# Eight modulation rows of a two-layer diffusion backbone, gathered in one PSUM bank and turned once

## The chip, the cores and the metric

The kernel runs on one core of one Trainium2 chip. The metric is device time in microseconds, from the first to the last instruction of one execution. The median of three runs of the kernel before is 1852.27 us (1848.69 to 1852.5). A core has five engines that run side by side, each with its own queue of instructions in a fixed order: PE (TensorE, matrix products), DVE (VectorE), ACT (ScalarE), POOL (GpSimd) and SP (SyncE, here only the issuer of most transfers). PE multiplies from SBUF, the working memory of 128 partitions, into PSUM, eight banks of 512 fp32 columns by 128 partitions.

## What is computed

A backbone of two layers over 1024 latent tokens and 256 context tokens, width 1024: layer 0 is windowed attention, layer 1 a bidirectional state-space mixer. Every layer is modulated by two condition vectors, c for the latent tokens and c_ctx for the context tokens:

```python
def adaln(cond, w, b):
    mod = jax.nn.silu(cond) @ w + b
    return jnp.split(mod, 3, axis=-1)
...
for i in range(DEPTH):
    shift, scale, gate = adaln(c, w_ada[i], b_ada[i])
    shift_c, scale_c, gate_c = adaln(c_ctx, w_ada[i], b_ada[i])
    u = rms_normalize(h) * (1.0 + scale[:, None]) + shift[:, None]
    ...
    h = h + gate[:, None] * y
```

For each layer this is a product of 2 x 1024 by 1024 x 3072, so six blocks of 512 output columns: blocks 0 and 1 are the shift, 2 and 3 the scale, 4 and 5 the gate. The products are computed in fp32. What uses them wants a modulation value as one number per partition, with the 128 features of a tile on the partitions. A product comes out the other way round, as two rows (c and c_ctx) of 512 columns, and so has to be turned.

## The kernel before

Most matrix products are made in three passes from a split of each fp32 operand into a high part (wh, uH) and a rest (wl, uL). `mm3` (L223 to L229) issues them: high by high (L227), high by rest (L228), rest by high (L229). The weights arrive by a transfer (wr, L220), ACT casts them to the high part (L213), DVE or POOL subtracts (L215).

Blocks 0 to 3 of layer 0 are needed at once and are made at the start (`ada0`, L361 to L371, tiles wada and arow). The other eight, blocks 4 and 5 of layer 0 and all six of layer 1, are made later, between the projections of layer 0, by `adaln_col`. One block is eight transfers of 256 KB (L181, k = 0 to 7, alternately four in the buffers wh and four in wl of the pool wv) and eight matmuls (L185). The weight operand of such a matmul is 32 columns wide (`cs32`: two columns with silu of c and c_ctx, 30 of zeros), so that four matmuls of a group stand side by side in the array, each writing one strip of 32 partitions of the bank `aps`. Two groups, k = 0 to 3 and k = 4 to 7, make one block. Then comes the ninth step, `fin`: ACT copies the bank to SBUF (L189, a buffer of the tag qf), `modulation` turns it by four matmuls of 128 x 128 slices against `sel` (L201, which also adds the four strips), DVE adds the bias (L203), and, by the block, one more DVE operation (L192 or L205). fp32 matmuls show two records each in the profile: a group of four is eight records of L185, a turning eight records of L201.

Which engine's queue holds what in which order is decided by the framework. It plans the whole kernel in simulated time from the program's order, places an instruction where it thinks its operands are ready, picks the buffer of a tag and sets the semaphores. The program only says in which order the steps are written down. Around the change that is `qkvg` (L551 to L607): after the k and v projections it runs eight rounds of q projections (x = 0 to 7, for each the context tokens, i = 2, and then the first 512 latent tokens, i = 0) and eight of g projections (i = 2 for all x, i = 0 for x = 4 to 7), and calls `fill` after each projection, which runs the next three, three, three or two steps of the list `ada`. With nine steps to a block the list has 72 steps.

The projections use the two qf buffers too: `rope` for a q or k of latent tokens (L501 to L504) and `g_out` (L541 to L543, the last being the transfer of the result, sg, to memory). Behind the last projection the pools wv, wq and qp are closed and the attention's pools att, wo and qp1 are opened in the same place of SBUF. A new tile waits for the last users of the bytes under it. The attention starts with transfers of cos and sin (L510, L511), q (L614, L620, on POOL's queue), sg (L616), and the weights of the projections of the other 512 latent tokens (L220, cast at L213), which run between the attention's blocks.

Of the kernel before, what the change touches and what calls it, by code (L numbers as in the profile page):

```python
# [9 lines left out]
F32 = mybir.dt.float32  # L10
# [3 lines left out]
ALU = mybir.AluOpType  # L14
# [3 lines left out]
P = 128  # L18
D = 1024
KT = D // P  # L20
# [22 lines left out]
    pj=1, S=2, pt=2, pv=1,  # L43
# [60 lines left out]
class Kernel:  # L104
# [52 lines left out]
    def load_cond(self, p):  # L157
        nc, t, cp = self.nc, self.t, self.cp
        cc = t(p, [P, KT, 2], F32, "cc")
        nc.sync.dma_start(cc, self.a["cc"].rearrange("p (k c) -> p k c", k=KT))  # L160
        th = t(p, [P, KT, 2], F32, "cth")
        nc.scalar.activation(th, cc, AF.Tanh, scale=0.5)
        nc.vector.tensor_scalar_mul(cc, cc, 0.5)
        cs = self.csf = t(cp, [P, KT, 2], F32, "cs")
        nc.vector.scalar_tensor_tensor(cs, in0=th, scalar=1.0, in1=cc, op0=ALU.add, op1=ALU.mult)

        self.sel = t(cp, [P, 2], F32, "sel")
        nc.vector.tensor_reduce(self.sel, self.ident.rearrange("p (j r) -> p r j", r=32)[:, 0:2], axis=mybir.AxisListType.X, op=ALU.add)
        self.bada = t(cp, [P, 2, 24], F32, "bada")
        nc.sync.dma_start(self.bada, self.a["bada"].rearrange("p (l t) -> p l t", l=2))  # L170

    def adaln_col(self, layer, n, pool, ps):

        nc, t = self.nc, self.t
        st = {}

        def step(k):
            if k == 0:
                st["ps"] = t(ps, [P, 512], F32, "aps", 2)
            raw = t(pool, [P, 4, P], F32, ("wh", "wl")[k // 4])  # L180
            nc.sync.dma_start(raw, self.a["w_ada"][layer, n, k].rearrange("p (a c) -> p a c", a=4))  # L181
            st[k] = raw
            if k % 4 == 3:
                for j in range(4):
                    nc.tensor.matmul(st["ps"][32 * j : 32 * j + 32], self.cs[:, k - 3 + j, :], st[k - 3 + j].rearrange("p a c -> p (a c)"), start=k == 3, stop=k == KT - 1)  # L185

        def fin():
            row = t(self.pq, [P, 512], F32, "qf")
            nc.scalar.copy(row, st["ps"])  # L189
            m = self.modulation(layer, n, row, ps)  # L190
            if n // 2 == 2 and layer == 0:
                nc.vector.tensor_scalar_mul(m, m, 0.5)  # L192

        return [lambda k=k: step(k) for k in range(KT)] + [fin]

    def modulation(self, layer, n, row, ps):

        nc = self.nc
        mt = self.t(ps, [P, 512], F32, "pt")
        for j in range(4):  # L200
            self.last_mod = nc.tensor.matmul(mt[:, 2 * j : 2 * j + 2], row[:, j * P : (j + 1) * P], self.sel, start=True, stop=True)  # L201
        m = self.mod[layer][:, n * 4 : n * 4 + 4, :]
        nc.vector.tensor_tensor(m, mt[:, :8].rearrange("p (a b) -> p a b", b=2), self.bada[:, layer, n * 4 : n * 4 + 4].unsqueeze(2).broadcast_to([P, 4, 2]), op=ALU.add)  # L203
        if n // 2 == 1:
            nc.vector.tensor_scalar_add(m, m, 1.0)  # L205
        return m
# [91 lines left out]
    def layer0(self):  # L298
        nc, t, a = self.nc, self.t, self.a
        cps = ExitStack()  # L300
        BUFS.update(S=1, pj=4, wr=7, qf=2, ql=2, wh=4, wl=4, sqt=2)
        self.psA = self.pool("psA", space=PSUM, ctx=cps)
        NB = (LAT + CTX) // P
        self.uH, self.uL = [None] * 3, [None] * 3
        cw = ExitStack()
        wvp = self.pool("wv", ctx=cw)

        self.cs = t(wvp, [P, KT, 32], F32, "cs32")
        nc.vector.memset(self.cs, 0.0)
        nc.vector.tensor_copy(self.cs[:, :, 0:2], self.csf)  # L310
        self.wp = self.pool("wq", ctx=cw)
        p = self.pq = self.pool("qp", ctx=cw)
        c0 = ExitStack()
        self.q_d = [[t(self.dr, [4, 2, HD, n], F32, f"q{j}_{i}") for i, (_, n) in enumerate(TT)] for j in range(KV)]
        self.sg_d = [[t(self.dr, [2, P, n], F32, f"sg{j}_{i}") for i, (_, n) in enumerate(TT)] for j in range(KV)]
        wk, wv = self.norm0(c0, p, wvp)
        c0.close()
        ckv = ExitStack()
        kvp = self.pool("kv", ctx=ckv, side="right")
        self.kHH = [t(kvp, [P, LAT + CTX], F32R, f"kHH{j}") for j in range(KV)]  # L320
        self.v = t(kvp, [P, NB, KV, 2 * HD], F32R, "v")
        self.kL = [t(kvp, [P, LAT + CTX], F32R, f"kL{x}") for x in range(KV // 2)]
        self.mask = t(kvp, [P, 1152], BF16, "mask")
        self.nsink = t(kvp, [P, HEADS], F32, "nsink")
        self.sink = t(kvp, [P, HEADS], F32, "sink")
        self.qkvg(p, wk, wv, wvp)
        if "u" in self.dump:
            for i, (s, n) in enumerate(TT):
                self.dump_split("u", self.uH[i], self.uL[i], i, n, s)
        cw.close()  # L330
        cps.close()
        with ExitStack() as c1:
            BUFS.update(S=2, pj=1)
            self.psA = self.pool("psT", space=PSUM, ctx=c1)
            self.attention(c1, ckv)
            BUFS.update(pj=2)
# [24 lines left out]
    def ada0(self, n, raw, ps):  # L361

        nc, t = self.nc, self.t
        pj = t(ps, [P, 512], F32, "aps", 2)
        for k in range(KT):
            j = k % 4
            mm = nc.tensor.matmul(pj[32 * j : 32 * j + 32], self.cs[:, k, :], raw[k // 2][:, k % 2], start=k < 4, stop=k >= 4)
        row = t(self.p0, [P, 512], F32, "arow")
        nc.scalar.copy(row, pj)
        self.modulation(0, n, row, ps)  # L370
        return mm, self.last_mod  # L371
# [179 lines left out]
    def qkvg(self, p, wk, wv, wvp):  # L551
        nc, t, a = self.nc, self.t, self.a
        ps = self.psA
        nc.gpsimd.dma_start(self.mask, a["mask"])
        nc.sync.dma_start(self.sink, a["sink"].broadcast_to([P, HEADS]))
        nc.vector.tensor_scalar_mul(self.nsink, self.sink, -1.0)
        v = self.v
        NB = (LAT + CTX) // P
        kh_d = [[t(self.dr, [P, n], F32, f"k{x}_{i}") for i, (_, n) in enumerate(TT)] for x in range(2)]

        def kproj(x, i):
            s, n = TT[i]
            h, _ = self.qk(p, self.proj_h(ps, wk[x], self.uH, self.uL, i), i, self.kL[x][:, s : s + n])
            nc.sync.dma_start(kh_d[x][i], h.bitcast(F32))
            for e in range(2):
                for hf in range(2):
                    nc.gpsimd.dma_start(self.kHH[2 * x + e][hf * HD : (hf + 1) * HD, s : s + n], kh_d[x][i][e * HD : (e + 1) * HD, :])

        def vproj(b):
            i = 0 if b < 4 else (1 if b < 8 else 2)  # L570
            o = (b * P) - TT[i][0]
            pj = t(ps, [P, 512], F32, "pj")
            self.mm3(pj[:, :256], [(self.uH[i][:, k, o : o + P], self.uL[i][:, k, o : o + P],
                                    wv[k // 2][0][:, k % 2, :], wv[k // 2][1][:, k % 2, :]) for k in range(KT)])
            pv = pj[:, :256].rearrange("p (j d) -> p j d", j=KV)
            nc.scalar.copy(v[:, b, :, :HD], pv)
            nc.vector.tensor_sub(v[:, b, :, HD:], pv, v[:, b, :, :HD])

        for i, (s, n) in enumerate(TT):
            kproj(0, i)  # L580
            if i:
                kproj(1, i)
            for b in range(s // P, (s + n) // P):
                vproj(b)
            if i == 0:
                kproj(1, i)
        ada = []
        for layer, n in [(0, 4), (0, 5)] + [(1, n) for n in range(6)]:
            ada += self.adaln_col(layer, n, wvp, ps)

        def fill(m):
            for f in ada[:m]:
                f()
            del ada[:m]

        n = [3, 3, 3, 2]
        for x in range(8):
            w = self.load_halves(a["wq"][x])
            for i in (2, 0):
                self.q_step(p, w, x, i)  # L600
                fill(n[x % 2 * 2 + (i == 0)])
        for x in range(8):
            w = self.load_halves(a["wg"][x])
            for i in (2, 0) if x >= G0 else (2,):
                self.g_step(p, w, x, i)
                fill(n[x % 2 * 2 + (i == 0)])
        fill(len(ada))  # L607
# [1022 lines left out]
```

## Time and profile before

| | |
|---|---|
| median of three runs | 1852.27 us (1848.69 to 1852.5) |
| the profiled execution | 1852.09 us, of it span of the instructions 1850.4 us |
| PE busy | 1764.7 us, 95% of the span |
| DVE, ACT, POOL busy | 63%, 48%, 43% |
| mean granted clock of PE | 0.988 of full speed |
| late w_ada transfers (L181) | 64 of 256 KB, 16.8 MB of 227.64 MB in all |
| late w_ada matmuls (L185) | 128 records, first at 142.6 us, last group at 263.8 us |
| late turnings (L201 on qf) | 64 records, first at 152.8 us, last at 268.7 us |

The profile shows one execution. Busy time is summed by engine; PE's loading of weights (PEld) runs beside its matmuls. Rows of the trace in order of time give the start in us, the length in us, the engine, the line of the kernel, the operation, the tile written and those read, and how many records are merged (x8); a bracket at the end gives how long the engine had been idle and what it waited for. Matmuls overlap, so the time that one takes from the stream is read from start to start, not from its length. SPq and POOLq are the queues that issue transfers: their rows show the issue, not the transfer.

### The profile page before, as it was taken

What the parts mean: (1) busy time and instruction counts of PE and PEld (TensorE: products, weight loads), DVE (VectorE), ACT (ScalarE), POOL (GpSimd) and SP (SyncE); (2) the same over time, 40 slices, a digit from 0 to 9 for tenths busy, and PEclk for the clock granted to TensorE, in tenths of its full rate; (3) what the DMA queues carried; (4) which work ended last, traced back from release to release, by engine and by line L of the source; (5) the groups of instructions that cost most, each with busy time, mean ns of one, the idle gap of its engine ahead of it and who ended that gap; (6) DMA issues with size and microseconds to landing.
All of it is one profiled execution on the core that took longest, in us unless ns stands there. A gap on an engine that the chain in (4) does not pass through costs nothing. (4 is left out here: it accounts for less than half of the span.)

```text
span 1850.4 us, 29176 instructions
## 1 busy us (share of the span) xinstructions
PE 1764.7 (95%) x10375; PEld 1506.2 (81%) x10375; DVE 1171.9 (63%) x2144; ACT 894.8 (48%) x1963; POOL 803.8 (43%) x1066
## 2 busy tenths in 40 slices
PE   6899998899999999989999999999999999999997
PEld 2697776788889687768889898988989898888886
DVE  4534426887777755684776757676675767766643
ACT  3812226677778765573443535344353534454422
POOL 2331107654456454202454554545455454554321
PEclk8999999999999999999999999999999999999998
DMA  8658856553355455321332333332232323455542
GB/s 313 233 135 254 250 160 150 132 124 88 95 129 131 105 147 169 127 67 43 83 74 78 81 77 78 80 89 69 77 93 65 86 72 99 150 170 166 177 137 69
DMA packets 212498, 227.64 MB, mean 123 GB/s; under 512 B 16384, under 2 KB 149632, under 8 KB 212352
## 3 DMA queue, kind: packets, MB, share of 16 engines
q1 hardware_dynamic: 178288, 207.12, 37.7%
q0 software_dynamic: 34064, 18.65, 5.6%
q8 instruction: 82, 1.34, 0.3%
q14 instruction: 64, 0.52, 0.1%
HBM read 190.88 MB, written 35.13 MB: 122 GB/s over the span
## 5 line engine op out<-in xcount | busy, mean ns | idle before, releaser
L227 PE MATMUL pj<-uH,wh 128*128 128x512 f32 (+1 forms) x712 | 257.7, 363 | 18.4 <-ACT uH L446 8.5
L228 PE MATMUL pj<-uL,wh 128*128 128x512 f32 (+1 forms) x712 | 244.9, 344 | 0.2 <-DVE uL L447 0.2
L229 PE MATMUL pj<-uH,wl 128*128 128x512 f32 (+1 forms) x712 | 244.2, 344 | 0.7 <-POOL wl L215 0.5
L1140 POOL TENSOR_TENSOR xw<-xn,dtdec 128x256 f32<-128x256 f32 x144 | 106.3, 741 | 197.2 <-PE psD L1165 125.0
L227 PEld LDWEIGHTS pj<-uH,wh 128*128 128x128 f32 x712 | 136.4, 192 | 48.1 <-issue 10.3
L1071 PE MATMUL pj<-uH,wh 128*128 128x512 f32 x512 | 165.6, 399 | 4.4 <-ACT bn L1025 2.4
L1071 PE MATMUL pj<-uL,wh 128*128 128x512 f32 x512 | 167.8, 401 | 1.1 <-DVE uL L291 1.1
L1071 PE MATMUL pj<-uH,wl 128*128 128x512 f32 x512 | 167.2, 401 | 0.7 <-DVE wl L1002 0.7
L215 POOL TENSOR_TENSOR wl<-wr,wh 128x512 fp32r<-128x512 f32 x92 | 123.0, 1341 | 88.3 <-ACT wh L213 87.8
L666 DVE TENSOR_TENSOR pl<-pt,ph 128x512 fp32r<-128x512 f32 x168 | 114.4, 687 | 66.3 <-ACT ph L665 65.5
L1096 PE MATMUL pj<-wh,uH 128*128 128x256 f32 x512 | 151.0, 295 | 2.6 <-ACT xn L1025 2.6
L228 PEld LDWEIGHTS pj<-uL,wh 128*128 128x128 f32 x712 | 137.0, 192 | 15.9 <-DVE uL L447 2.5
L229 PEld LDWEIGHTS pj<-uH,wl 128*128 128x128 f32 x712 | 135.9, 191 | 17.1 <-POOL wl L215 2.0
L1096 PE MATMUL pj<-wh,uL 128*128 128x256 f32 x512 | 149.1, 291 | 0.0
L1096 PE MATMUL pj<-wl,uH 128*128 128x256 f32 x512 | 146.4, 286 | 0.0
L213 ACT CAST wh<-wr 128x512 fp32r<-128x512 f32 (+1 forms) x132 | 84.7, 645 | 115.7 <-PE pj L228 83.2
L640 DVE CUSTOM_DVE_ANT_0 sm<-S,mask,nsink 128x640 f32<-128x640 f32 (+2 forms) x160 | 119.2, 771 | 21.4 <-PE S L637 13.6
L665 ACT CAST ph<-pt 128x512 fp32r<-128x512 f32 x168 | 97.4, 585 | 58.9 <-PE pt L661 55.3
L642 ACT ACTIVATE sm<-sm,nm 128x640 f32<-128x640 f32 (+2 forms) x160 | 118.7, 742 | 12.4 <-DVE nm L640 12.0
L1071 PEld LDWEIGHTS pj<-uH,wh 128*128 128x128 f32 x512 | 94.7, 189 | 25.0 <-ACT bn L1025 2.6
L1071 PEld LDWEIGHTS pj<-uL,wh 128*128 128x128 f32 x512 | 96.6, 189 | 21.9 <-DVE uL L291 2.0
L1071 PEld LDWEIGHTS pj<-uH,wl 128*128 128x128 f32 x512 | 96.4, 189 | 20.5 <-DVE wl L1002 1.1
(370 smaller groups left out, 4821.8 us busy)
## 6 DMA issues: line engine op xcount, KB each, us to landing
wr<-w_x SPq DMA_DIRECT2D x32, 512.0 KB, 5.2
M<-acs SPq DMA_DIRECT2D x64, 256.0 KB, 5.1
bw<-acs SPq DMA_DIRECT2D x64, 256.0 KB, 5.0
wr<-wo SPq DMA_DIRECT2D x48, 256.0 KB, 2.7
wr<-w_sk SPq DMA_DIRECT2D x24, 512.0 KB, 4.5
wr<-wg SPq DMA_DIRECT2D x40, 256.0 KB, 3.7
qs<-q POOLq DMA_DIRECT2D x40, 256.0 KB, 3.8
wada<-w_ada SPq DMA_DIRECT2D x16, 512.0 KB, 7.4
```

The lines of the kernel that those rows point to most:

```text
L213: nc.scalar.copy(h, raw)
L215: (eng or nc.vector).tensor_tensor(l, raw, h, op=ALU.subtract)
L227: self.nc.tensor.matmul(ps, lh, rh, start=first and i == 0, stop=False)
L228: self.nc.tensor.matmul(ps, lh, rl, start=False, stop=False)
L229: self.nc.tensor.matmul(ps, ll, rh, start=False, stop=last and i == n - 1)
L640: nc.vector.tensor_tensor_reduce(out=sm[:, :W], in0=Sv, in1=self.mask[:, m0 : m0 + W], scale=-SCALE, scalar=self.nsink[:, 4 * j + r : 4 * ...
L642: nc.scalar.activation(sm[:, :W], sm[:, :W], AF.Exp, bias=nm[:, r : r + 1], scale=-1.0, accum_out=sums[:, r : r + 1])
L665: nc.scalar.copy(ph, ptf)
L666: nc.vector.tensor_sub(pl, ptf, ph)
L1071: nc.tensor.matmul(raw[:, 512 * i : 512 * i + 512], l[:, k, :], r[i][:, k, :], start=k + y == 0, stop=k == KT - 1 and y == 2)
L1096: nc.tensor.matmul(pj[:, c], l, r[:, k, :], start=c % 2 + q + k + y == 0, stop=c % 2 == 1 and q == 1 and k == 3 and y == 2)
L1140: nc.gpsimd.tensor_tensor(xw, X(st, c).rearrange("p (r h) -> p r h", r=R), self.dtdec[:, c, hd(d, g)].unsqueeze(2).broadcast_to([P, R, HP] ...
```

## The change

The eight late blocks no longer have a bank and a turning each. All of them add into one bank. The tile with the condition's two columns is 46 columns wide (`cs46`), the two columns at 14 and 15, zeros around them. Block x takes the 32 columns from 14 - 2x on, so that its two values come out in rows 2x and 2x + 1 of each strip and zeros are added to the other rows. After the last block one copy, four matmuls against a `sel` of 16 columns, and four DVE operations give all eight blocks. A block is eight steps and the whole list 65. The matmuls of a group are issued in the order j = 3 to 0. The tile of a transfer is declared as 512 columns, and no longer as four times 128; the bytes are the same. `ada0` and `modulation` stay for the first four blocks and read slices of the wider tiles.

```diff
--- before.py
+++ after.py
@@ -164,41 +164,49 @@
         cs = self.csf = t(cp, [P, KT, 2], F32, "cs")
         nc.vector.scalar_tensor_tensor(cs, in0=th, scalar=1.0, in1=cc, op0=ALU.add, op1=ALU.mult)
 
-        self.sel = t(cp, [P, 2], F32, "sel")
-        nc.vector.tensor_reduce(self.sel, self.ident.rearrange("p (j r) -> p r j", r=32)[:, 0:2], axis=mybir.AxisListType.X, op=ALU.add)
+        self.sel = t(cp, [P, 16], F32, "sel")
+        nc.vector.tensor_reduce(self.sel, self.ident.rearrange("p (j r) -> p r j", r=32)[:, 0:16], axis=mybir.AxisListType.X, op=ALU.add)
         self.bada = t(cp, [P, 2, 24], F32, "bada")
         nc.sync.dma_start(self.bada, self.a["bada"].rearrange("p (l t) -> p l t", l=2))
 
-    def adaln_col(self, layer, n, pool, ps):
+    def ada1(self, pool, ps):
+
 
         nc, t = self.nc, self.t
-        st = {}
-
-        def step(k):
-            if k == 0:
-                st["ps"] = t(ps, [P, 512], F32, "aps", 2)
-            raw = t(pool, [P, 4, P], F32, ("wh", "wl")[k // 4])
-            nc.sync.dma_start(raw, self.a["w_ada"][layer, n, k].rearrange("p (a c) -> p a c", a=4))
-            st[k] = raw
+        order = [(0, 4), (0, 5)] + [(1, n) for n in range(6)]
+        raws = {}
+        aps = t(ps, [P, 512], F32, "aps", 2)
+
+        def step(s):
+            x, k = divmod(s, KT)
+            layer, n = order[x]
+            raws[s] = t(pool, [P, 512], F32, ("wh", "wl")[k // 4])
+            nc.sync.dma_start(raws[s], self.a["w_ada"][layer, n, k])
             if k % 4 == 3:
-                for j in range(4):
-                    nc.tensor.matmul(st["ps"][32 * j : 32 * j + 32], self.cs[:, k - 3 + j, :], st[k - 3 + j].rearrange("p a c -> p (a c)"), start=k == 3, stop=k == KT - 1)
+                for j in reversed(range(4)):
+                    nc.tensor.matmul(aps[32 * j : 32 * j + 32], self.cs[:, k - 3 + j, 14 - 2 * x : 46 - 2 * x], raws.pop(s - 3 + j), start=x == 0 and k == 3, stop=x == 7 and k == KT - 1)
 
         def fin():
             row = t(self.pq, [P, 512], F32, "qf")
-            nc.scalar.copy(row, st["ps"])
-            m = self.modulation(layer, n, row, ps)
-            if n // 2 == 2 and layer == 0:
-                nc.vector.tensor_scalar_mul(m, m, 0.5)
-
-        return [lambda k=k: step(k) for k in range(KT)] + [fin]
+            nc.scalar.copy(row, aps)
+            mt = t(ps, [P, 512], F32, "pt")
+            for j in range(4):
+                nc.tensor.matmul(mt[:, 16 * j : 16 * j + 16], row[:, j * P : (j + 1) * P], self.sel, start=True, stop=True)
+            v = mt[:, :64].rearrange("p (j n c) -> p n j c", n=8, c=2)
+            for layer, n0, i0, i1 in ((0, 4, 0, 2), (1, 0, 2, 8)):
+                m = self.mod[layer][:, 4 * n0 :].rearrange("p (n j) c -> p n j c", j=4)
+                nc.vector.tensor_tensor(m, v[:, i0:i1], self.bada[:, layer, 4 * n0 :].rearrange("p (n j) -> p n j", j=4).unsqueeze(3).broadcast_to([P, i1 - i0, 4, 2]), op=ALU.add)
+            nc.vector.tensor_scalar_mul(self.mod[0][:, 16:], self.mod[0][:, 16:], 0.5)
+            nc.vector.tensor_scalar_add(self.mod[1][:, 8:16], self.mod[1][:, 8:16], 1.0)
+
+        return [lambda s=s: step(s) for s in range(8 * KT)] + [fin]
 
     def modulation(self, layer, n, row, ps):
 
         nc = self.nc
         mt = self.t(ps, [P, 512], F32, "pt")
         for j in range(4):
-            self.last_mod = nc.tensor.matmul(mt[:, 2 * j : 2 * j + 2], row[:, j * P : (j + 1) * P], self.sel, start=True, stop=True)
+            self.last_mod = nc.tensor.matmul(mt[:, 2 * j : 2 * j + 2], row[:, j * P : (j + 1) * P], self.sel[:, :2], start=True, stop=True)
         m = self.mod[layer][:, n * 4 : n * 4 + 4, :]
         nc.vector.tensor_tensor(m, mt[:, :8].rearrange("p (a b) -> p a b", b=2), self.bada[:, layer, n * 4 : n * 4 + 4].unsqueeze(2).broadcast_to([P, 4, 2]), op=ALU.add)
         if n // 2 == 1:
@@ -305,9 +313,9 @@
         cw = ExitStack()
         wvp = self.pool("wv", ctx=cw)
 
-        self.cs = t(wvp, [P, KT, 32], F32, "cs32")
+        self.cs = t(wvp, [P, KT, 46], F32, "cs46")
         nc.vector.memset(self.cs, 0.0)
-        nc.vector.tensor_copy(self.cs[:, :, 0:2], self.csf)
+        nc.vector.tensor_copy(self.cs[:, :, 14:16], self.csf)
         self.wp = self.pool("wq", ctx=cw)
         p = self.pq = self.pool("qp", ctx=cw)
         c0 = ExitStack()
@@ -364,7 +372,7 @@
         pj = t(ps, [P, 512], F32, "aps", 2)
         for k in range(KT):
             j = k % 4
-            mm = nc.tensor.matmul(pj[32 * j : 32 * j + 32], self.cs[:, k, :], raw[k // 2][:, k % 2], start=k < 4, stop=k >= 4)
+            mm = nc.tensor.matmul(pj[32 * j : 32 * j + 32], self.cs[:, k, 14:46], raw[k // 2][:, k % 2], start=k < 4, stop=k >= 4)
         row = t(self.p0, [P, 512], F32, "arow")
         nc.scalar.copy(row, pj)
         self.modulation(0, n, row, ps)
@@ -584,9 +592,7 @@
                 vproj(b)
             if i == 0:
                 kproj(1, i)
-        ada = []
-        for layer, n in [(0, 4), (0, 5)] + [(1, n) for n in range(6)]:
-            ada += self.adaln_col(layer, n, wvp, ps)
+        ada = self.ada1(wvp, ps)
 
         def fill(m):
             for f in ada[:m]:
```

## Prediction

> **What bounds the kernel now.** I read the page first (busy shares and slices), then busy time by stage, then the instructions in order of time around one turning and around the end of the projections. The chain that ended last covers only the final 50 us and tells nothing about this place.
>
> ```profile
> span 1850.4 us, 29176 instructions
> PE 1764.7 (95%) x10375; PEld 1506.2 (81%) x10375; DVE 1171.9 (63%) x2144; ACT 894.8 (48%) x1963; POOL 803.8 (43%) x1066
> GB/s 313 233 135 254 250 160 150 132 124 88 95 129 131 105 147 169 127 67 43 83 74 78 81 77 78 80 89 69 77 93 65 86 72 99 150 170 166 177 137 69
> ```
>
> TensorE is the bound of the whole, at 95%. The changed steps run in slices 3 to 5 of 46 us each. By stage (columns: window, length, busy us and instructions of PE, PEld, DVE, ACT and POOL, granted clock, DMA share, GB/s):
>
> ```profile
> 142.60:274.20 131.60, 131.60 (x818) 102.78 (x817) 49.40 (x99) 32.26 (x61) 15.37 (x12) 1.00 0.72 222
> 142.00:245.00 103.00, 103.00 (x654) 79.77 (x652) 44.16 (x88) 27.81 (x52) 12.55 (x8) 1.00 0.80 253
> 215.00:230.00 15.00, 15.00 (x117) 11.71 (x116) 8.49 (x17) 6.29 (x12) 1.57 (x1) 1.00 0.91 287
> 281.60:285.70 4.10, 0.00 (x0) 0.00 (x0) 0.21 (x2) 0.64 (x2) 0.76 (x2) 0.63 1.75 282
> 285.70:289.50 3.80, 3.77 (x13) 3.19 (x14) 2.10 (x6) 3.33 (x11) 2.71 (x3) 0.50 0.37 87
> ```
>
> From the first late w_ada group (142.6) to the last projection (274.2, called E) PE is busy for 131.60 of 131.60 us at full clock. It waits for nothing there, so a microsecond taken off PE is a microsecond off E. Behind E attention begins, with one real hole: 4.1 us without a matmul, then 3.8 us at half clock.
>
> **The turnings: the main term.** Starts on PE around one turning (L201), around two that fell inside a group of w_ada matmuls (L185), and around a whole group:
>
> ```profile
> 152.58 0.39 PE L227 MATMUL pj<-uH,wh 128*128 128x512 f32 x1
> 152.81 0.95 PE L201 MATMUL pt<-sel,qf 128*128 128x2 f32 x8
> 153.62 0.49 PE L228 MATMUL pj<-uL,wh 128*128 128x512 f32 x1
> 153.94 0.40 PE L229 MATMUL pj<-uH,wl 128*128 128x512 f32 x1
> ...
> 187.81 1.04 PE L185 MATMUL aps<-wh,cs 128*32 128x512 f32 x2
> 188.79 1.05 PE L201 MATMUL pt<-sel,qf 128*128 128x2 f32 x8
> 189.77 1.06 PE L185 MATMUL aps<-wh,cs 128*32 128x512 f32 x6
> 190.76 0.50 PE L227 MATMUL pj<-uH,wh 128*128 128x512 f32 x1
> ...
> 252.36 1.06 PE L185 MATMUL aps<-wh,cs 128*32 128x512 f32 x6
> 253.35 1.05 PE L201 MATMUL pt<-sel,qf 128*128 128x2 f32 x8
> ...
> 142.61 1.07 PE L185 MATMUL aps<-wh,cs 128*32 128x512 f32 x8
> 143.61 0.39 PE L227 MATMUL pj<-uH,wh 128*128 128x256 f32 x1
> ```
>
> A matmul of 512 columns takes 0.23 us of the stream (152.58 to 152.81). L228 starts 0.81 after the turning, and L229 0.32 after L228, 0.09 more than 0.23: a turning costs 0.90 us. A whole group takes 1.00 (142.61 to 143.61). Cut by a turning it takes 190.76 - 187.81 = 2.95, so that turning costs 1.95; the one at 253.35 is cut the same way. L201 has 64 records here, eight to a turning, so eight turnings: 6 x 0.90 + 2 x 1.95 = 9.3 us.
>
> One turning is left, over the same four 128x128 slices of the row, by 16 columns now and not 2. A record takes 0.12 us now, far below the 0.23 of 512 columns, so 16 columns are nearest to 2: I keep 0.90 (bounds 0.90, and 8 x 0.23 = 1.84). It follows all groups and cannot cut one. **Gain on PE: 9.3 - 0.9 = 8.4 us**, 7.5 at the bound. Its matmuls wait for the copy of the bank, which before had its own wait:
>
> ```profile
> L189 ACT COPY qf<-aps 128x512 f32<-128x512 f32 x8 | 4.7, 587 | 6.4 <-DMA sg<-qf 4.1 <-PE aps L185 2.3
> ```
>
> Seven of these eight ACT copies go, and most of their 4.1 us of waiting for a store to free a qf buffer. ACT is busy for 32 of 131.6 us, and PE, never idle in this stage, waits for none of the eight copies, so this gains nothing; if the planner put the last turning right behind its copy, PE would wait once, at most these 4.1. DVE (busy 49.4) loses eight small adds and gets four larger ones, 64 columns at most; hidden as well.
>
> **Edits at the front.** sel gets 16 columns, the padded tile 368 columns to clear, not 256:
>
> ```profile
> 3.19 0.27 DVE L309 MEMSET cs<- 128x256 f32 x1
> 8.15 5.47 DVE L433 TENSOR_TENSOR sqa<-sqa,sqt 128x512 f32<-128x512 f32 x7 [4.47 <-ACT sqt L432]
> ```
>
> 0.27 x 368 / 256 = 0.39, so 0.12 us more, under 4.47 us in which DVE waits; without that cover, 0.12 us. L367 reads a slice of the wider tile with the same 32 columns: 0.
>
> **The groups.** 64 loads and 64 matmuls of the same shapes stay, in 16 groups. The zero columns add nothing but zeros, so one bank serves as two did: 0. The strips now start with the last loaded, so a group waits for its fourth load before it does anything. What decides is how far ahead the loads are:
>
> ```profile
> 143.69 1.77 SPq L181 DMA_DIRECT2D wh<-w_ada  x4
> 152.26 1.98 SPq L181 DMA_DIRECT2D wl<-w_ada  x4
> DMA to landing us min/median/max: 2.7/4.4/7.7
> ...
> 157.13 1.06 PE L185 MATMUL aps<-wh,cs 128*32 128x512 f32 x8
> 163.80 0.64 PE L185 MATMUL aps<-wl,cs 128*32 128x512 f32 x4
> 263.84 1.06 PE L185 MATMUL aps<-wl,cs 128*32 128x512 f32 x8
> ```
>
> The four loads issued until 145.46 serve the group at 157.13, those until 154.24 the one at 163.80: 11.7 and 9.6 us ahead. A block takes 8 steps and not 9 (65 in all, not 72) at the same three or two per projection, so by the code the last group follows x = 5, i = 2 of the g loop and not x = 6, i = 0. Ahead of it stand two 512-token projections and one of 256 fewer: 24 matmuls each at 0.23 us, and at half of it for half the columns, 2 x 5.5 + 2.9 = 13.9 us. The spacing of groups falls from (263.84 - 142.61) / 15 = 8.1 us to (121.2 - 8.4 - 13.9) / 15 = 6.6, and a load that runs two groups ahead loses 3.0 us: 8.7 and 6.6 are left, above the median landing of 4.4, and 1.1 under the longest, 7.7.
>
> The rate rises too. Behind the last w_ada load it is
>
> ```profile
> 245.00:268.00 23.00, 23.00 (x138) 18.00 (x137) 3.67 (x7) 4.17 (x8) 2.81 (x4) 1.00 0.39 111
> ```
>
> so 253 GB/s x 103 us = 26.1 MB, less 13.9 us x 111 GB/s = 1.5 MB that now come later, must pass in 103 - 6.5 - 13.9 = 82.6 us (six turnings lie before 245, one of them cut: 5 x 0.90 + 1.95 = 6.5): an estimate of 298 GB/s. The page shows 313 in slice 0, and the stages 287 at a share of 0.91 without PE waiting. If 287 were the ceiling, 24.6 MB would take 85.7 us, 3 us more. Bounds 0 to 3; nearer to 313, I take a loss of 1.0. [...]
>
> **The hole behind E.** Rows of PE, ACT and SP:
>
> ```profile
> 281.06 0.50 PE L668 MATMUL pv<-pl,v 128*128 128x512 f32 x1 [0.15 <-DVE pl L666]
> 285.73 0.80 PE L227 MATMUL pj<-uH,wh 128*128 128x512 f32 x1 [4.16 <-ACT wh L213]
> 285.06 0.62 ACT L213 CAST wh<-wr 128x512 fp32r<-128x512 f32 x1 [4.77 <-DMA wr<-wq]
> 268.88 0.32 SPq L543 DMA_DIRECT2D sg<-qf  x1
> 275.77 0.33 SPq L543 DMA_DIRECT2D sg<-qf  x1
> 277.94 0.35 SPq L510 DMA_DIRECT2D cos<-cos  x1
> 278.34 0.42 SPq L511 DMA_DIRECT2D sin<-sin  x1
> 278.81 10.56 SPq L220 DMA_DIRECT2D wr<-wq  x4
> ```
>
> PE waits for a cast, that for weights issued at 278.81, and these stand on SP behind cos, which goes 2.17 us after the last sg store: the time of a store to land. Why it waits for that store can be counted from the tile sizes. Per partition, each tile padded to 32 bytes, from the start of pool wv: wv and wq hold 17,408 + 30,720 bytes, then cos and sin 8,192, then two qf buffers of 2,048; the second lies at 58,368 to 60,416. Attention's pools att (42,688) and wo (16,384) put the new cos at 59,072 to 61,120, over that second buffer. Uses of qf before: 14 stores of sg, 12 rotations, 8 rows = 34; if the buffers alternate, the last store reads the second one. After: 27, so it reads the first. The wider tile moves the old buffers by 448: the second, 58,816 to 60,864, is still under cos, the first is not. So cos waits only for the store before (268.88 + 2.17 = 271.1 instead of 277.9), and wr, which lies over the wl buffers of wq, is free at E, when the last projection has left them. Issued at E + 0.3 instead of E + 4.6, landing after the same 6.25 us, cast and used 0.67 later (285.06 to 285.73): E + 7.2, before the hole opens at E + 7.4. The hole closes: **4.1 us**. The half clock behind it holds 3.8 x 0.5 = 1.9 us; attention's start waits for DVE and ACT too, so I take the middle, 1.0 (bounds 0 and 1.9). If wr stays behind the last store (E + 1.6 + 0.3), it is used at E + 9.1 and 2.4 us are won.
>
> [...]
>
> **Sum**, against the profiled execution (1852.1, 0.2 under the median 1852.27): 1852.1 - 8.4 + 1.0 - 4.1 - 1.0 = **1839.6**.
>
> **Rivals.**
> 1. The hole stays: a row that is released early breaks the alternation, or the planner keeps cos behind the last store. For it: the parity rests on one buffer order. 1852.1 - 8.4 + 1.0 = 1844.7.
> 2. The gain does not arrive. Attention's order is written by the planner from its own times; a shift by one buffer can bring one more hole like 281.6 (4.1 + 1.9 = 6.0): 1852.1 - 8.4 + 1.0 + 6.0 = 1850.7. Against it: nothing after E is tied to the clock on the wall, all of it moves with E.
> 3. Slower: late loads. Each of the 16 groups now stands still until its fourth load; at 1.1 us each (the longest landing) that is 17.6, and 1852.1 - 8.4 + 17.6 = 1861.3. It decides from 12.1 / 16 = 0.76 us a group. For it: 298 GB/s is near the highest rate seen, and SP issues loads in order. Against: landing is 4.4 in the middle, and the planner can place a group later.
>
> **How the numbers follow.** The forecast 0.48, rival 1 0.28, rival 2 0.12, rival 3 0.12. A measurement here tells about 0.2%, 3.7 us: faster means under 1848.6. The forecast, rival 1 and a third of rival 2 lie there: 0.80; same, the rest of rival 2: 0.08; slower 0.12. Low end: all of 8.4 + 4.1 + 1.9 gives 1837.7, less some 2 us for the spread of the runs shown (1848.69 to 1852.5): 1835.5. High end: rival 1 with 3 us of late loads is 1846.7, with the bound of the turning 1847.6: 1848. Outside stay rival 3 and most of rival 2, 0.2.
>
> **What would show it.** L201 on qf with 8 records, not 64; L189 once; no group cut. E near 266.8, PE still busy in every microsecond before it. L185 without waits for w_ada (with them: rival 3). SP issues cos before the last sg store, wr within 1 us of E, and no PE gap above 2 us behind E (otherwise rival 1). A new gap later in attention means rival 2. I am wrong altogether if E moves by less than 5 us.

## The result and the profile after

The changed kernel takes 1839.32 us (median of six executions, 1836.81 to 1842.58), the kernel before, run beside it, 1851.88 us (1847.52 to 1855.22). The ratio is 0.9942, with a 95% interval of 0.9926 to 0.9959: faster by 0.6%. The forecast was 1839.6. One execution of a kernel further down (`gpace`) took 4407.35 us; no trace shows it, and its ratio leaves it out.

The profiled execution after takes 1838.57 us. The head of its page and the line of transfer rates:

```profile
span 1836.6 us, 29048 instructions
PE 1753.6 (95%) x10319; PEld 1497.6 (82%) x10319; DVE 1169.8 (64%) x2136; ACT 891.8 (49%) x1956; POOL 800.9 (44%) x1066
GB/s 311 235 134 274 278 155 161 124 110 98 98 129 131 110 130 214 73 75 38 89 67 85 92 63 95 62 92 67 85 92 63 95 62 115 138 175 166 174 137 69
```

PE has 56 records fewer, which are the 56 of the seven turnings that went. Slices 3 and 4 now move 274 and 278 GB/s, not 254 and 250: the same loads in less time. The span is 13.8 us shorter. Where that lies is seen from two starts, in both profiles the same: the first late w_ada group (called g0: 142.61 us before, 142.60 after) and the first attention matmul E. In order of time on PE after, around the one turning that is left (now L194), and at E:

```profile
247.98 0.39 PE L235 MATMUL pj<-uH,wh 128*128 128x512 f32 x1
248.21 0.96 PE L194 MATMUL pt<-sel,qf 128*128 128x16 f32 x8
249.01 0.48 PE L236 MATMUL pj<-uL,wh 128*128 128x512 f32 x1
249.33 0.40 PE L237 MATMUL pj<-uH,wl 128*128 128x512 f32 x1
...
265.99 0.39 PE L237 MATMUL pj<-uH,wl 128*128 128x512 f32 x1
266.21 0.28 PE L643 MATMUL S<-kHH,qs 128*128 128x256 f32 x1
267.78 0.38 PE L643 MATMUL S<-kHH,qs 128*128 128x256 f32 x1 [1.29 <-DVE qf L550]
```

The same place before:

```profile
274.17 0.28 PE L637 MATMUL S<-kHH,qs 128*128 128x256 f32 x1
275.80 0.39 PE L637 MATMUL S<-kHH,qs 128*128 128x256 f32 x1 [1.35 <-DVE qf L542]
```

E comes at 266.21 instead of 274.17. The stretch from g0 to E fell from 131.56 to 123.61 us: 7.95 us less. The rest of the execution, E to the end, fell from 1850.4 - 274.17 = 1576.2 to 1836.6 - 266.21 = 1570.4: 5.8 us less. Both together are the 13.8.

Read the turning as in the prediction: 249.01 - 248.21 = 0.80, then 0.32 to L237, 0.09 above 0.23: 0.89 us. Sixteen columns cost what two did (0.89 against 0.90 us). The wait of 1.29 at 267.78 is not new; before it was 1.35 at the same place.

The busy time by stage of the profile after (columns: window, length, busy us and instructions of PE, PEld, DVE, ACT and POOL, granted clock, DMA share, GB/s):

```profile
142.60:266.20 123.60, 122.61 (x760) 95.42 (x760) 48.10 (x91) 28.23 (x54) 15.39 (x12) 1.00 0.74 236
220.00:230.00 10.00, 9.01 (x79) 7.39 (x75) 4.55 (x8) 3.50 (x8) 0.00 (x0) 1.00 0.95 307
266.20:269.60 3.40, 1.64 (x9) 1.04 (x8) 1.78 (x6) 1.30 (x4) 0.00 (x0) 1.00 0.26 87
269.60:273.20 3.60, 3.60 (x18) 3.06 (x17) 2.01 (x10) 2.37 (x9) 2.08 (x5) 0.53 0.92 287
```

PE is no longer busy in every microsecond of the stage: 122.61 of 123.60. The missing 0.99 us is one wait, in the ten microseconds with a DMA share of 0.95. Rows of the groups on PE and of the transfers on SP around it:

```profile
219.41 1.06 PE L187 MATMUL aps<-wl,cs 128*32 128x512 f32 x8
...
223.43 1.06 PE L187 MATMUL aps<-wh,cs 128*32 128x512 f32 x8
...
229.81 1.06 PE L187 MATMUL aps<-wl,cs 128*32 128x512 f32 x8 [0.99 <-DMA wl<-w_ada]
...
221.68 0.33 SPq L551 DMA_DIRECT2D sg<-qf  x1
222.34 0.33 SPq L184 DMA_DIRECT2D wl<-w_ada  x1
222.99 0.33 SPq L551 DMA_DIRECT2D sg<-qf  x1
223.65 1.29 SPq L184 DMA_DIRECT2D wl<-w_ada  x3
```

The group at 229.81 was due at 228.82; the last of its loads went out by 224.94, 3.9 us ahead. It could not go before the group of 219.41 had left the four wl buffers, and in SP's order two sg stores stand among the loads.

The hole behind E is gone. SP after, and the cast and the first matmul of the next projection, which end the chain that had made the hole. That matmul is called the first fill matmul below, since these projections fill the gaps of the attention; the function `fill` is something else:

```profile
267.75 0.33 SPq L551 DMA_DIRECT2D sg<-qf  x1
268.27 0.35 SPq L518 DMA_DIRECT2D cos<-cos  x1
...
269.16 8.98 SPq L228 DMA_DIRECT2D wr<-wq  x4
...
273.05 0.62 ACT L221 CAST wh<-wr 128x512 fp32r<-128x512 f32 x1 [0.19 <-DMA wr<-wq]
...
273.64 0.50 PE L674 MATMUL pv<-pl,v 128*128 128x512 f32 x1
273.98 0.40 PE L235 MATMUL pj<-uH,wh 128*128 128x512 f32 x1
```

cos stands 0.52 us behind the last store instead of 2.17, so it no longer waits for that store to land. E to the first fill matmul is 7.77 us (before 285.73 - 274.17 = 11.56), and from E to that matmul the longest PE gap is now the one at the very start (1.29). Half clock is not gone: it comes at 269.6 to 273.2 instead of 285.7 to 289.5.

### The profile page after: what moved, and what is told of

It reads as the page before. It is cut to its first block, busy times and chain, and to the rows that moved or that the text cites. A ratio compares the mean times of both kernels' runs of the same rounds, so it can differ in the third digit from the quotient of the medians.

```text
span 1836.6 us, 29048 instructions
## 1 busy us (share of the span) xinstructions
PE 1753.6 (95%) x10319; PEld 1497.6 (82%) x10319; DVE 1169.8 (64%) x2136; ACT 891.8 (49%) x1956; POOL 800.9 (44%) x1066
## 5 line engine op out<-in xcount | busy, mean ns | idle before, releaser
L237 PE MATMUL pj<-uH,wl 128*128 128x512 f32 (+1 forms) x712 | 243.7, 343 | 0.2 <-POOL wl L223 0.2
L237 PEld LDWEIGHTS pj<-uH,wl 128*128 128x128 f32 x712 | 135.5, 190 | 17.2 <-POOL wl L223 0.9
L646 DVE CUSTOM_DVE_ANT_0 sm<-S,mask,nsink 128x640 f32<-128x640 f32 (+2 forms) x160 | 118.7, 771 | 19.9 <-PE S L643 12.5
```

The source lines that it names most:

```text
L237: self.nc.tensor.matmul(ps, ll, rh, start=False, stop=last and i == n - 1)
L646: nc.vector.tensor_tensor_reduce(out=sm[:, :W], in0=Sv, in1=self.mask[:, m0 : m0 + W], scale=-SCALE, scalar=self.nsink[:, 4 * j + r : 4 * ...
```

## The experiments

Eleven more runs were made, of seven edited kernels: after2 and after3 repeat the changed kernel, parity2 repeats parity_back, gpace2 repeats gpace. Totals are ratios against the kernel before, run beside each of them. Since the executions of one kernel spread by 3 to 11 us, the finer readings are times within a profile: the stage from g0 to E, the PE waits in it, and E to the first fill matmul.

| kernel | ratio (95%) | stage, us | waits for w_ada in it | E to first fill, us |
|---|---|---|---|---|
| before | 1 | 131.56 | none | 11.56 |
| after | 0.9942 (0.9926 to 0.9959) | 123.61 | 0.99 | 7.77 |
| 1 turn8 | 0.9949 (0.9931 to 0.9967) | 129.56 | 0.66 | 10.38 |
| 2 before_flip | 0.9965 (0.9952 to 0.9977) | 131.55 | none | 7.42 |
| 3 parity_back | 0.9930 (0.9911 to 0.9950) | 123.39 | 0.77 | 10.75 |
| 4 aps_last | 0.9926 (0.9910 to 0.9942) | 124.31 | 1.76 | 7.48 |
| 5 before_rev | 0.9999 (0.9985 to 1.0014) | 130.43 | none | 14.31 |
| 6 pace | 0.9932 (0.9907 to 0.9956) | 122.95 | 0.32 | 8.29 |
| 7 after2 | 0.9914 (0.9889 to 0.9939) | 126.43 | 2.30 | 7.78 |
| 8 parity2 | 0.9935 (0.9910 to 0.9961) | 126.13 | 1.95 | 9.87 |
| 9 gpace | 0.9908 (0.9887 to 0.9929) | 122.45 | none | 7.59 |
| 10 gpace2 | 0.9926 (0.9903 to 0.9950) | 122.45 | none | 7.70 |
| 11 after3 | 0.9930 (0.9911 to 0.9948) | 123.75 | 1.13 | 7.91 |

**What a turning costs.** The changed kernel with its one turning issued eight times over, all behind the last group:

```diff
-            mt = t(ps, [P, 512], F32, "pt")
-            for j in range(4):
+            for y in range(32):
+                j = y % 4
+                if j == 0:
+                    mt = t(ps, [P, 512], F32, "pt")
```

> The changed kernel with the four matmuls of the last turning issued eight times over, into banks of the tag pt of which only the last is read; nothing is left out. If a turning costs the stream 0.90 to 1.00 us and PE is the bound here, the first attention matmul moves from 266.2 to 272.5 to 273.2 and the total by the same 6.3 to 7.0 us, ratio 0.998. If turnings were hidden beside other work (rival), the first attention matmul moves by less than 2 us and the ratio stays at 0.994.

Without its wait the stage takes 129.56 - 0.66 = 128.90, after 123.61 - 0.99 = 122.62: seven more turnings cost 6.28 us, 0.90 each. That is the price taken in the prediction. E itself stands at 268.54 and not later because g0 came 3.6 us sooner in this profile. E to the first fill matmul rose to 10.38, which the added turnings do not explain by themselves; its cause stays open. The total did not follow as expected, 0.9949 (0.9931 to 0.9967) and not 0.998: in the profile E to the end is 2.0 us shorter than after (1568.4 against 1570.4). So the price of a turning is shown for the stage, and not that all of it reaches the end.

**The parity of the qf buffers.** The kernel before with the row of its last block alone in a buffer of another tag, so that qf is used 33 times and not 34; and the changed kernel with its row in that tag, 26 uses and not 27:

```diff
-            row = t(self.pq, [P, 512], F32, "qf")
+            row = t(self.pq, [P, 512], F32, "rope_b" if (layer, n) == (1, 5) else "qf")
...
-            row = t(self.pq, [P, 512], F32, "qf")
+            row = t(self.pq, [P, 512], F32, "rope_b")
```

> The kernel before, with the row of the last block alone in a buffer of the tag rope_b, so that qf has 33 uses and the last store reads the first buffer; all eight turnings stay, nothing is left out. Theory of the buffers: the first attention matmul stays at 274.2 us, cos goes 0.5 us behind the last store, weights about 1.7 us earlier and ahead of the next q transfers, the hole of 4.1 us closes: 4 to 6 us faster than before, ratio 0.997 (0.9965 to 0.998). Rival (the hole belongs to the denser loads or the planner): hole of 4 us as before, ratio 1.000.

> The changed kernel, with the one copied row in a buffer of the tag rope_b, so that qf has 26 uses and the last store of sg reads the second qf buffer again; nothing is left out. Theory of the buffers: the first attention matmul stays at 266.2 us (within 0.3), but cos again waits for the last store to land, about 2.1 us behind it and not 0.5; the weights of wq follow at E + 4.6, behind the next q transfers, and a stretch of 3 to 4 us without a matmul comes back behind the first attention block. Total 4 to 6 us above the changed kernel, ratio to the kernel before 0.9965 (0.995 to 0.998). Rival (the hole closed because of a new order of the planner or because the late loads end earlier, the buffer has no part in it): cos and PE as in the changed kernel, ratio 0.994.

The wait of cos for the store can be read directly. Among SP's waits (us in total, times, longest) before, and with the parity put back:

```profile
SPq L510 <- DMA sg<-qf: 1.7, 1, 1.7
```

```profile
SPq L518 <- DMA sg<-qf: 1.6, 1, 1.6
```

After and with the flip there is no such wait. SP and PE of the kernel before with the flip, where E is 268.89:

```profile
270.44 0.33 SPq L543 DMA_DIRECT2D sg<-qf  x1
270.95 0.35 SPq L510 DMA_DIRECT2D cos<-cos  x1
...
271.83 8.23 SPq L220 DMA_DIRECT2D wr<-wq  x4
...
276.31 0.50 PE L227 MATMUL pj<-uH,wh 128*128 128x512 f32 x1
```

and of the changed kernel with the parity put back, where E is 259.54:

```profile
261.08 0.33 SPq L551 DMA_DIRECT2D sg<-qf  x1
263.12 0.35 SPq L518 DMA_DIRECT2D cos<-cos  x1
...
264.05 7.96 SPq L228 DMA_DIRECT2D wr<-wq  x3
...
266.98 0.51 PE L674 MATMUL pv<-pl,v 128*128 128x512 f32 x1
270.29 0.80 PE L235 MATMUL pj<-uH,wh 128*128 128x512 f32 x1 [2.80 <-ACT wh L221]
```

One row in another buffer, and nothing else, takes the hole out of the kernel before: cos goes 0.51 us behind the store, the wait of 4.16 for the cast is gone, and the kernel is 0.35% faster with eight turnings still in it (E to the end 1571.3 us and not 1576.2). The same edit in the changed kernel brings the 2.04 us between store and cos back, and a PE wait of 2.80. So the hole hung on the parity, and the change closed it by the way. In the total the reverse cannot be told: 0.9965 was expected and 0.9930 came, beside 0.9942, and 0.9935 beside 0.9914 on the chip of the repetition (parity2 and after2). In the profiles E to the end is longer by 4.2 us (1574.6 against 1570.4) and by 1.4 (1571.6 against 1570.2).

> The changed kernel with the copied row in a rope_b buffer once more. Theory of the buffers: stage 123.5 us, first fill matmul 10.5 to 11 us behind the first attention matmul, total 3 to 5 us above the changed kernel of the same chip. Rival (the hole is given back later, as the total of the first run says): same trace at the boundary, total within 1.5 us of the changed kernel.

> The changed kernel once more, beside the next one on the same chip, since the part before the first late w_ada matmul has scattered from 136.2 to 142.6 us between profiles with the same order of instructions. Stage 123.6 us again (within 0.5), first fill matmul 7.8 us behind the first attention matmul, ratio 0.994 (0.992 to 0.996).

In these two, E to the first fill matmul is 9.87 and 7.78: the hole is there with the one parity and not with the other, for the second time, smaller (a PE wait of 1.93 us). cos again waits for the store, 1.6 us, in parity2 alone.

The landing of the weights also went with the order of two queues. In the profiles before and with the parity put back, the next q transfer on POOL's queue (277.98 and 263.30) is issued before the weights (278.81 and 264.05), and the wait for them ends 6.25 and 5.57 us after their issue; in those after and with the flip the weights go first (269.16 before 269.96, 271.83 before 272.65), and it is 3.89 and 3.81 us. Over all thirteen profiles, from the issue to the first cast, it is less sharp: 3.6 to 4.6 us in the nine with the weights first, 4.7 to 6.3 in the four with the q transfer first (before, before_rev, parity_back, parity2). The order of the queues alone was not tried.

**The new wait for w_ada.** Two causes were possible: the reversed order of the strips, by which a group starts with its last load, or the denser loads. The order alone was put into the kernel before, and the loads of the changed kernel were spread in two ways: by one step less behind every second pair of projections (`pace`), and by two steps instead of three behind each of the short g projections, x = 0 to 3 with 256 tokens (`gpace`).

```diff
-                for j in range(4):
+                for j in reversed(range(4)):
...
-        n = [3, 3, 3, 2]
+        n = [3, 2, 3, 2]
...
                 self.g_step(p, w, x, i)
-                fill(n[x % 2 * 2 + (i == 0)])
+                fill(n[x % 2 * 2 + (i == 0)] if x >= G0 else 2)
```

> The kernel before with only the order of the four strips reversed in the late groups (the last loaded first); eight turnings, nothing is left out. Counted from the first late w_ada matmul to the first attention matmul, the stage is 131.56 us before. If the cut groups come from the order of the strips, no group is cut, and 2 x 1.05 = 2.1 us go: 129.5 us. If they come from the turnings alone, the stage stays at 131.5. The qf buffers are as before, so the hole of 4 us behind the projections stays. Total between 0 and 2 us faster, ratio 0.999.

> The changed kernel with three, two, three and two steps of the list after a projection and not three, three, three and two; nothing is left out. If the wait of 0.99 us for a w_ada load comes from the denser loads, it goes and the stage falls from 123.61 to 122.6 us; if it comes from the strips' order, it stays. Total within 1 us of the changed kernel, ratio 0.993 to 0.994.

> The changed kernel, with two w_ada transfers instead of three behind each of the four short g projections (x = 0 to 3, 256 tokens); the rest follows at x = 4 to 6. Nothing is left out. Theory (the new wait of a w_ada group, 0.66 to 2.30 us in the changed kernel and its variants, comes from three transfers behind each projection of half length): the wait goes or stays under 0.3 us, first late group to first attention matmul takes 123.61 - 0.99 = 122.6 us, and the time is 0 to 2 us below that of the changed kernel, 1836 to 1840. Rival (the wait comes from the w_ada transfers standing behind the sg stores on SP, however many there are): 0.6 to 2.3 us stay at some group, the stage takes 123.3 us or more, and the time is that of the changed kernel.

The order of the strips makes no wait and no measurable difference (0.9999). It leaves one cut group instead of two, and a stage shorter by 1.13; behind E the hole is longer (14.31 to the first fill matmul), and the gain is lost there. The density makes the wait: `pace` has 0.32 us, `gpace` nothing. The stage of `gpace`, and the transfers of the group that answers to 229.81:

```profile
136.36:258.81 122.45, 122.45 (x760) 95.37 (x760) 48.13 (x91) 27.97 (x54) 15.40 (x12) 1.00 0.75 238
```

```profile
213.16 1.06 PE L187 MATMUL aps<-wl,cs 128*32 128x512 f32 x8
...
220.01 1.07 PE L187 MATMUL aps<-wh,cs 128*32 128x512 f32 x8
...
229.54 1.06 PE L187 MATMUL aps<-wl,cs 128*32 128x512 f32 x8
...
216.90 0.38 SPq L184 DMA_DIRECT2D wl<-w_ada  x1
217.37 0.40 SPq L551 DMA_DIRECT2D sg<-qf  x1
217.87 1.46 SPq L184 DMA_DIRECT2D wl<-w_ada  x3
```

PE is busy for 122.45 of 122.45 us. The last load is issued by 219.33, 10.2 us ahead of its group and not 3.9, and the sg store among the loads does no harm. In the changed kernel the same wait stands in each profile (0.99, 2.30, 1.13), and with 2.30 it costs more than itself: the stage is 126.43, where 123.6 was expected again. Group and windows of that profile (after2):

```profile
224.97 1.25 PE L187 MATMUL aps<-wl,cs 128*32 128x512 f32 x8 [2.30 <-DMA wl<-w_ada]
```

```profile
220.00:230.00 10.00, 7.70 (x48) 6.34 (x47) 2.40 (x5) 2.18 (x5) 0.00 (x0) 0.83 0.96 335
220.00:240.00 20.00, 17.70 (x109) 13.38 (x108) 4.96 (x9) 4.35 (x10) 0.84 (x1) 0.91 0.76 251
```

The clock falls behind the wait: 0.91 over 20 us is 1.8 us of lost work.

The lighter pacing was run a second time beside the changed kernel, on one chip:

> The same kernel as the one with two transfers behind each short g projection, run on the same chip as the changed kernel. Theory (only the wait of the w_ada group is taken off): no wait of a w_ada group, the stage from the first late group to the first attention matmul takes 122.5 us again, and the time is 1 to 3 us below that of the changed kernel beside it. Rival (the lower time seen once was the scatter of the front of the kernel): the two medians differ by less than 1 us, or the other way round.

> The changed kernel again, beside the one with two transfers behind each short g projection. Theory (the load arrives late in each execution, by a varying amount): one w_ada group waits again, 0.7 to 2.3 us, and the stage takes 123.4 to 126.4 us, 1 to 4 more than with the lighter pacing. Rival (the wait is a matter of the chip): no wait, stage 122.6 us.

The stage repeats (122.45, no wait, against 123.75 with 1.13). The totals do not tell the two apart: 1837.2 us (1830.1 to 1841.08) and 1836.41 us (1832.97 to 1839.68). The first time `gpace` had 1833.26, the lowest median of all. So the loss of 1 to 4 us in the stage is taken away in both profiles; that the whole kernel is faster by it is not shown.

**The wait at the start of attention.** The second attention matmul waits 1.29 us for DVE to read the bank of the last projection (267.78). The last g projection was put in a bank of another tag:

```diff
-        self.g_out(p, self.proj_h(self.psA, w, self.uH, self.uL, i), x, i)
+        BUFS.update(aps=2)
+        self.g_out(p, self.proj_h(self.psA, w, self.uH, self.uL, i, "aps" if (x, i) == (7, 0) else "pj"), x, i)
```

> The changed kernel with the last g projection written to a bank of the tag aps, which lies idle by then, and not to the bank that the attention's second score tile takes over; nothing is left out. If the start of attention is held by that bank, the wait of 1.3 us of the second score matmul for the last gate operation goes and PE keeps busier in the 3.4 us behind E: 1.3 us faster than the changed kernel, up to 3 us if the stretch at half clock behind it (269.6 to 273.2) goes too, ratio 0.993. Rival: the chain of scores over DVE and ACT sets this start, the wait only moves, gain under 0.5 us.

```profile
264.44 0.41 PE L644 MATMUL S<-kL,qz 128*128 128x256 f32 x2
266.18 0.38 PE L644 MATMUL S<-kHH,qs 128*128 128x256 f32 x1 [1.32 <-DVE nm L647]
```

The wait is not saved but moved: the first four matmuls go at once, and PE then waits 1.32 us for nm, DVE's next step of the attention. The time is that of the changed kernel.

## Why the prediction was right

- **Turnings, -8.4.** Right in mechanism and price. The stage without its new wait is 131.56 - 122.62 = 8.94 shorter; against `gpace`, which has no wait, 9.11. Of that, turn8 gives 7 x 0.90 = 6.3. The two cuts, each put at 1.05 above a plain turning, cost 1.13 where one alone was taken away (before_rev). With two of these, 8.6 us are accounted for; 0.4 to 0.6 I cannot assign.
- **Sixteen columns cost as two.** Right: 0.89.
- **Denser loads, +1.0 (0 to 3).** 0.99 in the profile shown, but the stages of the six profiles whose loads are paced as in the change and whose last turning is untouched, less 122.45, give 1.16 (after), 3.98 (after2), 1.30 (after3), 0.94 (parity_back), 3.68 (parity2) and 1.86 (aps_last). The bound of 3 was too low. The step that failed is the average: I took 6.6 us from group to group everywhere and found 6.6 us of lead. Behind the short g projections groups stand 4.02 apart (219.41 to 223.43), and the lead there is 3.9, under the landing of the wl loads in that stretch, 3.5/4.9/5.5 us (shortest, median, longest). The spacing of 4.02 alone is not what is new, it stands at 162.74 to 166.76 too, without a wait. But a group's buffers are those of the group before the last, and between these two starts lie only 228.82 - 219.41 = 9.4 us here; everywhere else, and everywhere in `gpace`, it is 10.7 or more. A ceiling of the rate was also the wrong picture: 335 GB/s pass in the window of after2.
- **The hole, -4.1.** The count of buffers and bytes was right, and so was the size: E to the first fill matmul fell by 3.79, and by 4.14 with the parity alone. The way there was not as I had it. I expected cos ahead of the last store and wr within 1 us of E. The order on SP is the planner's, and it kept cos behind the store, so wr went at E + 2.95. The weights then arrived in 3.89 us and not in 6.25, and this made up for most of the delay. That is luck: with 6.25 from 269.16 the fill matmul would have come at E + 9.9, and 1.7 us would have been won. By its own signs (cos ahead of the last store, wr within 1 us of E) the prediction would have called this rival 1. Its fallback for wr behind the last store, E + 9.1, is also added up wrongly: 1.6 + 0.3 + 6.25 + 0.67 = 8.8.
- **Half clock, -1.0.** Not as I had it. The term was my estimate, about half of 3.8 x 0.5 us, and that the half clock would go with the hole no run shows: with the hole closed it is still there, earlier (0.53 over 3.6 us), and where it now stands it costs next to nothing. `gpace` and `gpace2` are the same kernel; in the same place behind E the one has full clock and the other has not:

```profile
262.20:265.80 3.60, 3.22 (x20) 2.26 (x18) 2.69 (x11) 2.18 (x9) 2.48 (x6) 1.00 0.93 296
```

```profile
267.80:271.40 3.60, 3.60 (x18) 3.02 (x17) 2.23 (x10) 2.24 (x8) 2.18 (x5) 0.60 0.97 283
```

E to the first fill matmul (7.59 and 7.70) and E to the end (1571.6 and 1571.7) differ by 0.1. From before to after, E to the end is 5.84 shorter, 3.79 of it in front of the first fill matmul; the other 2.05 come later, and no run assigns them to the clock.

- **No loss after E.** Right: the 13.8 us that the last instruction has gained were 14.1 in the middle of the attention (the uH casts, L683 before and L689 after, from 385 to 623 us).

Rival 1 (1844.7) was the change with the hole left in. parity_back and parity2 show that state: at the first fill matmul they lie 2.98 and 2.09 us behind the changed kernel, less than the 5.1 that I gave the hole and its half clock. Rival 3 had its mechanism right, late loads, but for one group and not sixteen.

The sum was 12.5 us, and 13.8 came in the profiled executions: 8.4 - 1.0 against 7.95, and 4.1 + 1.0 against 5.84. The medians lie 12.56 apart. The two main terms stand on their mechanisms, but that the total met the forecast to 0.3 us is luck: the executions of the two kernels spread by 6 to 8 us, the fast landing made up for the late issue, and 2.05 us from elsewhere stand where the 1.0 of the half clock was put.

## What to carry to other kernels

Here the work taken off PE, which never waited in the stage (131.60 of 131.60 us busy before), came off the end of that stage at the price read from start to start: 8.4 us were counted, 8.94 went without the new wait, and seven turnings put back cost 6.28. How much of it reaches the end of the kernel has to be measured: of the 6.3 us that turn8 added to the stage, 2.0 came back behind E in its profile. When work goes, ask which transfer is denser at its tightest place, not on average: look for the shortest work between two groups and give it fewer loads. And count the uses of every rotating buffer that a change touches: here, with two buffers, one use less in the kernel before took a PE wait of 4.16 us away, and one use less in the changed kernel brought one of 2.80 back.

## What the runs showed of the hardware that was not expected

**Half clock followed short gaps, and not each of them.** After E, in the changed kernel, PE was busy for 1.64 of 3.40 us, with no gap above 1.3 us in the brackets, and half clock followed (0.53 over the next 3.6 us). Behind single waits of 1.95 and 2.30 us inside a busy stage the clock was lower too (0.91 over 220 to 240 us in parity2 and after2); with one of 1.76 (aps_last) the stage is 1.86 longer than that of gpace, so almost nothing was lost beside the wait. The length of a gap alone does not decide: a gap of 1.84 us in the attention of the changed kernel, up to 315.70, was followed by full clock (1.00 from 315.70 to 320.00). Nor does the thin start. In `gpace` it had the same longest gap of 1.29 us (up to 260.38), and the clock stayed; before, PE was as thin (1.47 of 3.30 us), and the clock stayed too:

```profile
274.20:277.50 3.30, 1.47 (x8) 0.92 (x7) 1.66 (x6) 1.18 (x4) 0.00 (x0) 1.00 0.21 79
277.50:281.60 4.10, 3.70 (x20) 2.42 (x19) 3.19 (x13) 2.23 (x9) 2.84 (x6) 1.00 0.71 155
```

In the hole before, the mean clock was 0.63 over the 4.10 us. If that is made of the 1.00 and 0.50 of the rows beside it, an estimate is 3.0 of the 4.10 us at half. So in these runs the same gap of 1.29 us was followed by half clock in one profile (after) and by full clock in another (gpace); what decides was not shown.

**The front makes a good part of the spread of the totals.** Two profiles of the same kernel, gpace and gpace2, have the same stage (122.45) and the same E to the end (1830.4 - 258.81 = 1571.6, 1836.1 - 264.42 = 1571.7), and spans 5.7 us apart, 5.6 of it in front of g0. Most of that, 4.4 us, has come by the first matmul of the first projection, which waits 0.79 us in the one and 5.71 in the other. PE of the one and of the other:

```profile
27.23 1.22 PE L235 MATMUL pj<-uH,wh 128*128 128x512 f32 x2 [0.79 <-ACT uH L454]
```

```profile
31.59 1.22 PE L235 MATMUL pj<-uH,wh 128*128 128x512 f32 x2 [5.71 <-ACT uH L454]
```

The profiles before and after shown here both have the 5.71. The front is not the only source: over the three profiles of the changed kernel it spreads by 6.1 us, the stage by 2.8 and E to the end by 3.1. What decides in the front was not tried. The DMA share is 1.06 there, in the window after, 10 to 24 us:

```profile
10.00:24.00 14.00, 12.61 (x50) 4.69 (x50) 6.38 (x11) 4.01 (x9) 1.03 (x1) 1.00 1.06 385
```

385 GB/s is also more than the prediction reckoned with: it named 313 as the highest rate in the page, which was the average of a slice of 46 us. The profile before has 381 in the same window.
